# GLA's decayed keys and queries made in steps: from 4 tokens to 16, 64 and 128 by factors of a block

## The chip, the core and the metric

The program runs on one NeuronCore of a Trainium2 chip. Its engines are TensorE (PE; its weight loads are listed as PEld), VectorE (DVE), ScalarE (ACT), GpSimd (POOL) and SyncE (SP, which here only issues DMAs). Each engine works through its own list of instructions in order. The metric is the device time of one execution in microseconds (us); the kernel before takes 1629.36 us (median of 3 runs, 1627.66 to 1630.39).

## The reference

Two layers over 1024 tokens of width 1024: layer 0 mixes tokens by gated linear attention (GLA, 4 heads, key width 128, value width 512), layer 1 by a Mamba-2 mixer. Only GLA is touched. Within a chunk, with `b` the running sum of the log decays,

```python
    b = jnp.cumsum(ai, axis=-2)
    o_inter = jnp.einsum('bhcd,bhdv->bhcv', qi * jnp.exp(b), S)
    rel = jnp.where(causal, b[:, :, :, None, :] - b[:, :, None, :, :], -jnp.inf)
    attn = jnp.sum(qi[:, :, :, None, :] * ki[:, :, None, :, :] * jnp.exp(rel), axis=-1)
    o = o_inter + jnp.einsum('bhij,bhjv->bhiv', attn, vi)
    S = jnp.exp(b_last[:, :, 0, :, None]) * S + jnp.einsum(
        'bhjd,bhjv->bhdv', ki * jnp.exp(b_last - b), vi)
```

The sum over `d` has a decay that depends on both tokens and on `d`. It becomes a matmul only if the decay is split into a part for the key and a part for the query, each measured from a token between the two, so that neither exponential overflows.

## The kernel before

The 1024 tokens go in two halves of 512 (t = 0, 1); the first half meets each weight for the first time and splits it, the second loads the low part that the first has saved. GLA's work is the stage up to about 800 us of the span: four heads for t = 0, then four for t = 1. Every large product has three matmuls (high times high, low times high, high times low, lines 223 to 225 and 469 to 471). ACT makes a weight's high part `wh` (line 171), POOL its low part `wl` (line 176), or a DMA brings it. These matmul units of 12 run one behind the other, and a generator per head, `mixer(h)`, advances about one `yield` per unit beside them, so that its own small work falls between them. A scheduler that estimates times then fixes each engine's list; the kernel's `yield`s set the priorities.

A mixer projects the gate (z, line 540), makes `b` by four scans on DVE (line 551), and from `b`, the keys `k` and the queries `q` in a layout of 128 channels by 512 tokens: the keys decayed to the end of the chunk of 128 (`kd`, lines 558 to 560), the queries from its start (`qd`, 563 and 564), keys and queries about the chunk's middle (`d`, 569 to 573), keys to the end of each 16 and each 4 tokens (`keys`, 579 to 581), and queries against the end of each earlier 16, 4 or 1 tokens (`queries`, 597 to 601, with a copy on POOL for single tokens). Each takes a subtraction on DVE, an exponential on ACT and a multiplication on DVE; the tile names show up in the profile as `t`, `x`, `o` and `raw`, and `b` as `m`. PE then transposes `kd` (line 626), multiplies keys by queries (line 655), DVE places the results by masks (616, 620), and the attention and the state follow (705, 706, 712). At its end a mixer takes the norm over 512 values (line 293 on PE, 299 to 313 on DVE) and writes its output in four pieces `u` (line 738 on DVE), times the gate (739, POOL), rounded to `yh` and `yl` (743 on ACT, 744 on DVE), which the output projection reads. While one mixer ends, the next begins. DVE also carries values and gates out of PSUM (lines 480 and 419): a matmul that needs the bank waits for that.

## Time and profile before

| | us |
|---|---|
| median of the runs (lowest, highest) | 1629.36 (1627.66, 1630.39) |
| the profiled execution, whole time | 1634.13 |
| its span, first to last instruction | 1632.4 |
| PE busy | 1580.0 |
| DVE, ACT, POOL busy | 984.5, 947.2, 692.8 |

The profiled execution lies 4.8 us above the median of the runs. A matmul's busy time is modelled, and consecutive matmuls overlap. "Idle before" and a releaser name what ended an engine's wait. TensorE's granted clock is given as a share of 2.4 GHz.

### The profile page before, as it was taken

Reading aid. Unit: us, or ns where it says so; the run is one execution under the profiler, and the core shown is the slowest. Engines: PE = TensorE matmul, PEld = TensorE weight load, DVE = VectorE, ACT = ScalarE, POOL = GpSimd, SP = SyncE. Lnnn points to the kernel's source line nnn. Section 1 sums busy time; section 2 is a strip of 40 time slices with the busy share of each in tenths; the row PEclk is TensorE's granted clock in tenths of the full one; section 3 lists DMA queues with packets and bytes.
Section 4 is the critical chain, followed back from the end, with each engine's and each line's share of the span. In section 5 each row is a group of like instructions: output and inputs, shape, how many; then the busy total and the mean of one; then the engine's idle time right before and its main releaser. Section 6 shows DMA issues by size and latency. Waiting matters only on the chain.

```text
span 1632.4 us, 23995 instructions
## 1 busy us (share of the span) xinstructions
PE 1580.0 (97%) x8272; PEld 1308.2 (80%) x8272; DVE 984.5 (60%) x1579; ACT 947.2 (58%) x1788; POOL 692.8 (42%) x542
## 2 busy tenths in 40 slices
PE   7998999999999999999999999999999999999996
PEld 5777887877887888878888888887878888888886
DVE  6457567495736436295855534467885973355657
ACT  4435364543726355464874766665757777667843
POOL 6457566563412121126545655665523232222322
PEclk9999999999999999999999999999999999999999
DMA  7634556364585556463587555566666776656762
GB/s 232 185 123 131 176 174 201 123 201 146 191 269 193 162 166 217 154 207 120 176 262 228 175 188 173 173 209 216 208 193 186 257 235 221 204 177 189 260 197 84
DMA packets 172746, 309.30 MB, mean 189 GB/s; under 512 B 19088, under 2 KB 25104, under 8 KB 172624
## 3 DMA queue, kind: packets, MB, share of 16 engines
q1 hardware_dynamic: 172624, 307.77, 59.2%
q8 instruction: 65, 1.06, 0.3%
q14 instruction: 57, 0.47, 0.1%
HBM read 232.06 MB, written 75.63 MB: 188 GB/s over the span
## 4 chain that ended last, share of the span: by engine, by line
PE 78%; DVE 11%; ACT 4%; DMA 3%; issue 2%; POOL 2%; SPq 0%; DVEq 0%; ACTq 0%; POOLq 0%
PE pp L223 19%; PE pp L225 19%; PE pp L224 19%; PE pp L469 3%; PE pp L470 3%; PE pp L471 3%; PE mb L953 2%; PE mb L706 2%; DMA wraw<-w_in 2%; PE mb L705 2%; PE mb L946 1%; PE mb L655 1%; POOL wl L176 1%; PE mb L224 1%; PE mb L223 1%
## 5 line engine op out<-in xcount | busy, mean ns | idle before, releaser
L171 ACT CAST wh<-wraw 128x512 fp32r<-128x512 f32 x472 | 289.3, 618 | 379.3 <-PE pp L224 154.2
L223 PE MATMUL pp<-hh,wh 128*128 128x512 f32 x1184 | 468.3, 396 | 13.2 <-ACT wh L171 7.5
L176 POOL TENSOR_TENSOR wl<-wraw,wh 128x512 fp32r<-128x512 f32 x240 | 352.6, 1478 | 268.6 <-ACT wh L171 233.7
L224 PE MATMUL pp<-hl,wh 128*128 128x512 f32 x1184 | 464.1, 392 | 1.6 <-DVE hl L371 1.3
L225 PE MATMUL pp<-hh,wl 128*128 128x512 f32 x1184 | 463.2, 392 | 0.0
L223 PEld LDWEIGHTS pp<-hh,wh 128*128 128x128 f32 x1184 | 222.8, 188 | 65.3 <-ACT wh L171 9.0
L224 PEld LDWEIGHTS pp<-hl,wh 128*128 128x128 f32 x1184 | 222.9, 188 | 49.2 <-DVE hl L371 3.2
L225 PEld LDWEIGHTS pp<-hh,wl 128*128 128x128 f32 x1184 | 222.8, 188 | 46.5 <-issue 0.3
L223 PE MATMUL pp<-yh,wh 128*128 128x512 f32 x448 | 180.5, 403 | 5.2 <-DVE sg L419 2.4
L225 PE MATMUL pp<-yh,wl 128*128 128x512 f32 x448 | 178.5, 399 | 4.6 <-POOL wl L176 4.6
L224 PE MATMUL pp<-yl,wh 128*128 128x512 f32 x448 | 177.3, 396 | 0.0
L321 POOL TENSOR_TENSOR ss<-ss,t 128x512 f32<-128x512 f32 x53 | 74.4, 1403 | 81.7 <-ACT t L320 70.4
L223 PEld LDWEIGHTS pp<-yh,wh 128*128 128x128 f32 x448 | 85.6, 191 | 26.2 <-issue 4.5
L225 PEld LDWEIGHTS pp<-yh,wl 128*128 128x128 f32 x448 | 85.6, 191 | 24.4 <-POOL wl L176 5.1
L469 PE MATMUL pp<-wh,hh 128*128 128x512 f32 x256 | 100.8, 395 | 2.7 <-DVE m L444 2.7
L470 PE MATMUL pp<-wl,hh 128*128 128x512 f32 x256 | 101.0, 394 | 0.0
L471 PE MATMUL pp<-wh,hl 128*128 128x512 f32 x256 | 100.3, 394 | 0.0
L224 PEld LDWEIGHTS pp<-yl,wh 128*128 128x128 f32 x448 | 85.4, 191 | 18.2
L824 DVE SCALAR_TENSOR_TENSOR m<-pp,pr,m 128x509 f32<-128x509 f32 (+2 forms) x96 | 70.3, 742 | 40.0 <-ACT m L821 38.9
L824 DVE SCALAR_TENSOR_TENSOR x<-pp,pr,x 128x509 f32<-128x509 f32 (+2 forms) x96 | 71.2, 743 | 33.3 <-ACT x L821 32.2
L645 POOL TENSOR_TENSOR t<-v,t 128x512 fp32r<-128x512 f32 x28 | 40.6, 1460 | 101.5 <-ACT t L644 65.7
L739 POOL TENSOR_TENSOR t<-t,sg 128x512 f32<-128x512 f32 x32 | 50.9, 1621 | 75.3 <-ACT sg L98 68.3
(284 smaller groups left out, 2654.0 us busy)
## 6 DMA issues: line engine op xcount, KB each, us to landing
wraw<-w_in SPq DMA_DIRECT2D x352, 256.0 KB, 3.5
low_in<-wl SPq DMA_DIRECT2D x176, 256.0 KB, 3.8
wl<-low_in SPq DMA_DIRECT2D x176, 256.0 KB, 3.4
wraw<-w_out SPq DMA_DIRECT2D x128, 256.0 KB, 3.6
low_out<-wl SPq DMA_DIRECT2D x64, 256.0 KB, 4.3
v<-a_cum SPq DMA_DIRECT2D x64, 256.0 KB, 3.8
wl<-low_out SPq DMA_DIRECT2D x56, 256.0 KB, 3.4
xn<-x SPq DMA_DIRECT2D x43, 256.0 KB, 3.8
```

The lines of the kernel that those rows point to most:

```text
L171: A.copy(hi[:, 0:w], raws[n][:, 0:w])
L176: G.tensor_tensor(lo[:, 0:w], raws[n][:, 0:w], hi[:, 0:w].bitcast(F32), op=ALU.subtract)
L223: PE.matmul(o, lh, rh, start=first, stop=False)
L224: PE.matmul(o, lh, rl, start=False, stop=False)
L225: PE.matmul(o, ll, rh, start=False, stop=last)
L321: eng.tensor_tensor(ss, ss, sq, op=ALU.add)
L469: PE.matmul(o, rh[kb][:, cs], wh[:], start=(kb == 0), stop=False)
L470: PE.matmul(o, rh[kb][:, cs], wl[:], start=False, stop=False)
L471: PE.matmul(o, rl[kb][:, cs], wh[:], start=False, stop=(kb == KB - 1))
L645: G.tensor_tensor(vl, v[c], vh.bitcast(F32), op=ALU.subtract)
L739: G.tensor_tensor(u, u, self.g[h][vb], op=ALU.mult)
L824: V.scalar_tensor_tensor(dst[:, s:], o[:, 0:T - s], col(C_CW + j * 32 + si), dst[:, s:], op0=ALU.mult, op1=ALU.add)
```

## The change

`b` is turned into decays only over 4 tokens (and single tokens, as before). The keys to the end of 4 tokens, `k4`, are multiplied by a factor for each 4 tokens to give those to the end of 16, `k16`, and these by a factor for each 16 to give `kd` and the key half of `d`. The queries go the same way, in the tiles `t4` and `t16` (names `o1` and `o0`): queries from the last 4-token end, copies of them further back (`later`), then 16, then `qd` and the query half of `d`. The factors, 472 values per channel, are differences of `b` at block ends. POOL makes them: a copy of the ends (`ends`) and twelve small subtractions and copies per head; one exponential on ACT turns all of them into factors (`f`). The masks' placing keeps its instructions.

```diff
+            G.tensor_copy(ends[:, :, 1:9], b16[:, :, :, 15])
+            start, end = ends[:, :, 0:8], ends[:, :, 1:9]
...
+            fk = less(factors(NC, 8, 4), end.unsqueeze(3).to_broadcast([P, NC, 8, 4]), b4)
+            fq = factors(NC, 8, 4)
+            less(fq[:, :, :, 0], start, start)
+            less(fq[:, :, :, 1:4], b4[:, :, :, 0:3], start.unsqueeze(3).to_broadcast([P, NC, 8, 3]))
+            fkd = less(factors(NC, 8), ends[:, :, 8:9].to_broadcast([P, NC, 8]), end)
...
+            fqd = factors(NC, 8)
+            G.tensor_copy(fqd, start)
+            act(f[:, 0:at0[0]], f[:, 0:at0[0]], AF.Exp, scale=1.0 / 16)
...
+            k4 = tmp()
+            V.tensor_tensor(four(k4), bv[:, :, 3:4].to_broadcast([P, P, 4]), bv, op=ALU.subtract)
+            act(k4, k4, AF.Exp, scale=1.0 / 16)
+            yield
...
+            V.tensor_tensor(t4[:, :, 1:4, :], b5[:, :, 1:4, :], b5[:, :, 0:3, 3:4].to_broadcast([P, 32, 3, 4]),
+                            op=ALU.subtract)
+            V.tensor_tensor(t4[:, :, 0, :].rearrange("p (c j) l -> p c j l", c=NC), b16[:, :, :, 0:4],
+                            start.unsqueeze(3).to_broadcast([P, NC, 8, 4]), op=ALU.subtract)
+            act(t4[:, :, 0:4, :], t4[:, :, 0:4, :], AF.Exp, scale=1.0 / 16)
+            times(k4, k, k4)
+            k16 = tmp()
+            times(four(k16), four(k4), fk.rearrange("p c j m -> p (c j m)").unsqueeze(2).to_broadcast([P, P, 4]))
+            yield
             kd = tmp()
-            V.tensor_tensor(c3(kd), bc[:, :, P - 1:P].to_broadcast([P, NC, P]), bc, op=ALU.subtract)
-            act(kd, kd, AF.Exp, scale=1.0 / 16)
-            V.tensor_tensor(kd, k, kd, op=ALU.mult)
-            yield
-            qd = tl("x", 4)[:]
-            act(qd, b, AF.Exp, scale=1.0 / 16)
-            V.tensor_tensor(qd, q, qd, op=ALU.mult)
...
+            times(kd.rearrange("p (c j l) -> p c j l", c=NC, j=8), k16.rearrange("p (c j l) -> p c j l", c=NC, j=8),
+                  fkd.unsqueeze(3).to_broadcast([P, NC, 8, 16]))
+            times(t4[:, :, 0:4, :], q.rearrange("p (n m l) -> p n m l", m=4, l=4), t4[:, :, 0:4, :])
+            yield
...
+            times(t16[:, :, 0:4, :].rearrange("p n m (i l) -> p n m i l", l=4),
...
+            later(t4, f4, 4)
+            yield
...
-            k16, q16 = keys(16), queries(16, flat[0])
+            q1 = [singles(tl("raw", 2, (P, N_RAW))[:], 0, 2)]
             yield
...
-            k4, q4 = keys(4), queries(4, flat[1])
...
-            q1 = [queries(1, tl("raw", 2, (P, N_RAW))[:], 2 * i, 2 * i + 2) for i in range(2)]
+            q1.append(singles(tl("raw", 2, (P, N_RAW))[:], 2, NC))
```

A mixer has three `yield`s more between the scans and the products of keys and queries, so its later parts, and the end of a mixer against the beginning of the next, stand elsewhere in the lists. In the list after, line 535 is 532 before, 543 is 540, 554 is 551, 296 is 293, 700 is 626 and 724 is 655; `times` is line 599 and `less` line 577. The lists of the Mamba stage are the same.

First place: DVE's list, t = 1, the end of the third head's mixer (names `o_1268`, `o_1269` before) beside the copies of the fourth head's values `v` out of PSUM. Before:

```order
L313 SCALAR_TENSOR_TENSOR rstd_6519<-t_6523,t_6520 128x512
L738 SCALAR_TENSOR_TENSOR t_6550<-o_1268_5921,pr,rstd_6519 128x512
L738 SCALAR_TENSOR_TENSOR t_6575<-o_1268_5921,pr,rstd_6519 128x512
L738 SCALAR_TENSOR_TENSOR t_6609<-o_1269_5922,pr,rstd_6519 128x512
L738 SCALAR_TENSOR_TENSOR t_6634<-o_1269_5922,pr,rstd_6519 128x512
L480 COPY v_6599<-pp_6390 128x512
L480 COPY v_6603<-pp_6392 128x512
```

And now:

```order
L483 COPY v_6583<-pp_6358 128x512
L483 COPY v_6587<-pp_6360 128x512
L302 TENSOR_SCALAR t_6589<-mb_6559 128x512
L314 TENSOR_TENSOR t_6595<-t_6589,t_6592 128x512
L315 SCALAR_TENSOR_TENSOR t_6595<-t_6595,t_6592 128x512
L316 SCALAR_TENSOR_TENSOR rstd_6591<-t_6595,t_6592 128x512
L807 SCALAR_TENSOR_TENSOR t_6622<-o_1265_5902,pr,rstd_6591 128x512
```

The two copies stood behind the four `u`; now they stand ahead of the norm and of all four. Between the first and second and the second and third head of t = 1 they have moved in the same way.

Second place: DVE's list, t = 0, third head, up to the last instruction of `kd`, which is `t_2284` before and `t_2361` after. Before (the subtraction of `t_2284` is the fourth instruction behind the scans):

```order
L564 TENSOR_TENSOR x_2308<-m_376_1870,x_2308 128x512
L321 TENSOR_TENSOR ss_2191<-ss_2191,t_2319 128x512
L601 TENSOR_TENSOR raw_2448<-m_376_1870,raw_2448 128x64x3
L601 TENSOR_TENSOR raw_2448<-m_376_1870,raw_2448 128x64x2
L419 TENSOR_TENSOR sg_2280<-pp_2201,rstd_261 128x512
L560 TENSOR_TENSOR t_2284<-m_389_1930,t_2284 128x512
```

And now (`t_2285` is `f`, `t_2331` is `k16`, `o_478` is `t16`, `o_479` is `t4`):

```order
L617 TENSOR_TENSOR o_479_2326<-m_459_2242,ends 128x32x4
L599 TENSOR_TENSOR raw_2538<-m_365_1821,raw_2538 128x64
L599 TENSOR_TENSOR t_2298<-m_381_1882,t_2298 128x512
L599 TENSOR_TENSOR o_479_2326<-m_365_1821,o_479_2326 128x32x16
L599 TENSOR_TENSOR t_2331<-t_2298,t_2285 128x512
L599 TENSOR_TENSOR o_478_2325<-o_479_2326,t_2285 128x8x64
L599 TENSOR_TENSOR o_479_2326<-o_479_2326,t_2285 128x32x8
L599 TENSOR_TENSOR o_479_2326<-o_479_2326,t_2285 128x32x4
L422 TENSOR_TENSOR sg_2413<-pp_2346,rstd_263 128x512
L599 TENSOR_TENSOR t_2361<-t_2331,t_2285 128x512
```

`kd` now stands behind the single tokens' queries, `k4`, `t4`, `k16` and `t16`, and from `t_2331` on every instruction needs POOL's factors.

Third place: POOL's list, t = 0, second head. Before, low parts of weights follow one another; only the copy for single tokens stands between:

```order
L176 TENSOR_TENSOR wl_1364<-wraw_1283,wh_1363 128x512
L176 TENSOR_TENSOR wl_1393<-wraw_1312,wh_1392 128x512
L176 TENSOR_TENSOR wl_1422<-wraw_1337,wh_1421 128x512
L603 COPY raw_1551<-m_180_917 128x64x4
L176 TENSOR_TENSOR wl_1463<-wraw_1369,wh_1462 128x512
```

And now:

```order
L563 COPY ends<-m_281_1361 128x4x8
L577 TENSOR_TENSOR t_1392<-m_281_1361 128x64
L577 TENSOR_TENSOR t_1392<-m_281_1361 128x32
L179 TENSOR_TENSOR wl_1409<-wraw_1304,wh_1408 128x512
L577 TENSOR_TENSOR t_1392<-ends,m_281_1361 128x128
L577 TENSOR_TENSOR t_1392<-ends 128x32
L577 TENSOR_TENSOR t_1392<-m_281_1361,ends 128x32x3
L577 TENSOR_TENSOR t_1392<-ends 128x32
L577 TENSOR_TENSOR t_1392<-ends 128x16 x3
L577 TENSOR_TENSOR t_1392<-ends 128x8
L594 COPY t_1392<-ends 128x32
L179 TENSOR_TENSOR wl_1437<-wraw_1336,wh_1436 128x512
```

The copy of `ends` needs the scans on DVE, and every `wl` behind it now stands behind that. PE first needs `wl_1409` 99 matmuls of 512 columns behind the norm's matmul of the first head's mixer.

On PE, in matmuls of 512 columns, the lists have these distances to the transposes of `kd` and to the products of keys and queries, counted from the gate's projection z in the first head of t = 0 and from the norm's matmul of the mixer that ends in the other heads:

| head | transposes, products before | now |
|---|---|---|
| t = 0, first | 68, 88 | 79, 80 |
| t = 0, second | 112, 137 | 133, 170 |
| t = 0, third | 130, 171 | 134, 171 |
| t = 0, fourth | 122, 171 | 134, 171 |
| t = 1, second to fourth | 122 or 123, 171 | 134, 171 |

The output projection first reads `yh` 135 matmuls behind the norm's matmul before and 98 behind it now, for the first three heads of t = 1.

## Rows read from the trace of the kernel before

**Rows 1.** The page: busy time, share of the span and instructions of each engine; and the chain that ended last, its shares by engine.

```profile
PE 1580.0 (97%) x8272; PEld 1308.2 (80%) x8272; DVE 984.5 (60%) x1579; ACT 947.2 (58%) x1788; POOL 692.8 (42%) x542
...
PE 78%; DVE 11%; ACT 4%; DMA 3%; issue 2%; POOL 2%; SPq 0%; DVEq 0%; ACTq 0%; POOLq 0%
```

**Rows 2.** A stretch of 50 us that holds PE's longest wait in GLA's stage: its length, then PE busy (instructions), PEld, DVE, ACT, POOL, the granted clock, the DMA share and GB/s.

```profile
150.00:200.00 50.00, 45.34 (x256) 37.36 (x255) 35.09 (x70) 18.65 (x37) 30.64 (x20) 0.93 0.51 163
```

**Rows 3.** Who PE waited for in the whole run: us in total, times, longest us.

```profile
PE pp L225 <- POOL wl L176: 4.6, 1, 4.6
PE pp L223 <- DVE v L480: 4.2, 3, 1.4
PE mb L655 <- DVE raw L601: 3.4, 1, 3.4
...
PE mb L626 <- DVE t L560: 2.4, 2, 1.4
PE pp L223 <- DVE sg L419: 2.4, 2, 2.0
PE pp L223 <- DVE acc L515: 1.7, 2, 1.3
...
PE mb L655 <- DVE t L581: 0.5, 1, 0.5
...
PE mb L223 <- DVE a L620: 0.5, 1, 0.5
```

**Rows 4.** PE in order of time, start and us: the first head's z and the norms of the first three heads (t = 0); then, for t = 1, the third head's norm, the fourth's z, 37 matmuls behind it, and the matmul after that.

```profile
69.30 0.39 PE L540 MATMUL mb<-stp,wup 128*128 128x512 f32 x1
...
132.16 0.39 PE L293 MATMUL mb<-t,onr 128*128 128x512 f32 x1
...
217.01 0.39 PE L293 MATMUL mb<-t,onr 128*128 128x512 f32 x1
...
313.46 0.39 PE L293 MATMUL mb<-t,onr 128*128 128x512 f32 x1
...
688.74 0.39 PE L293 MATMUL mb<-t,onr 128*128 128x512 f32 x1
...
697.17 0.39 PE L540 MATMUL mb<-stp,wup 128*128 128x512 f32 x1
698.96 0.47 PE L223 MATMUL pp<-hh,wh 128*128 128x512 f32 x1 [1.41 <-DVE v L480]
```

**Rows 5.** DVE in order of time, fourth head of t = 1, where POOL has nothing to do: start and us of a group.

```profile
705.03 0.73 DVE L597 TENSOR_TENSOR raw<-m 128x192 f32<-128x192 f32 x3
705.67 0.68 DVE L558 TENSOR_TENSOR t<-m 128x512 f32<-128x512 f32 x1
706.28 0.68 DVE L569 TENSOR_TENSOR t<-m 128x512 f32<-128x512 f32 x1
...
707.48 2.09 DVE L597 TENSOR_TENSOR o<-m 128x384 f32<-128x384 f32 x6
...
715.38 0.85 DVE L601 TENSOR_TENSOR raw<-m,raw 128x192 f32<-128x192 f32 x3
```

**Rows 6.** DVE in order of time, t = 0: the first head from behind the scans to its last queries, and the scans of the second, third and fourth head.

```profile
74.26 1.78 DVE L597 TENSOR_TENSOR raw<-m 128x192 f32<-128x192 f32 x3
...
88.96 4.02 DVE L601 TENSOR_TENSOR raw<-m,raw 128x192 f32<-128x192 f32 x3
...
148.92 2.02 DVE L551 TENSOR_TENSOR_SCAN m<-t,t 128x128 f32<-128x128 f32 x4
...
236.36 2.58 DVE L551 TENSOR_TENSOR_SCAN m<-t,t 128x128 f32<-128x128 f32 x4
...
331.73 1.86 DVE L551 TENSOR_TENSOR_SCAN m<-t,t 128x128 f32<-128x128 f32 x4
```

**Rows 7.** POOL in order of time: the first head of t = 0 behind the scans, then the second; last, the one instruction of DVE in that second stretch that reads PSUM.

```profile
74.09 1.33 POOL L176 TENSOR_TENSOR wl<-wraw,wh 128x512 fp32r<-128x512 f32 x1 [0.63 <-ACT wh L171]
79.11 8.78 POOL L176 TENSOR_TENSOR wl<-wraw,wh 128x512 fp32r<-128x512 f32 x3 [3.68 <-ACT wh L171]
88.84 1.34 POOL L176 TENSOR_TENSOR wl<-wraw,wh 128x512 fp32r<-128x512 f32 x1 [0.96 <-DVE o L601]
90.14 2.71 POOL L645 TENSOR_TENSOR t<-v,t 128x512 fp32r<-128x512 f32 x2
...
152.35 10.78 POOL L176 TENSOR_TENSOR wl<-wraw,wh 128x512 fp32r<-128x512 f32 x3 [2.29 <-PE pp L225]
...
158.96 0.68 DVE L419 TENSOR_TENSOR sg<-pp,rstd 128x512 f32<-128x512 f32 x1
```

**Rows 8.** POOL's groups by line and shape, whole run: us busy, mean ns of one, idle before.

```profile
L176 POOL TENSOR_TENSOR wl<-wraw,wh 128x512 fp32r<-128x512 f32 x240 | 352.6, 1478 | 268.6 <-ACT wh L171 233.7 <-PE pp L225 9.2 <-DMA wraw<-w_in 7.0
...
L838 POOL TENSOR_TENSOR m<-m,heads 128x3 f32<-128x3 f32 x16 | 3.6, 227 | 51.5 <-DVE m L824 51.5
...
L834 POOL TENSOR_TENSOR heads<-halo,pr 128x96 f32<-128x96 f32 x1 | 0.4, 361 | 3.8 <-ACT halo L827 3.8
```

**Rows 9.** DVE in order of time, t = 1, the four `u` of the third head and the two copies behind them.

```profile
693.40 4.81 DVE L738 SCALAR_TENSOR_TENSOR t<-o,pr,rstd 128x512 f32<-128x512 f32 x4
698.14 1.28 DVE L480 COPY v<-pp 128x512 f32<-128x512 f32 x2
```

More of the change, by code (lines that the diff above doesn't have):

```diff
@@ L584, in queries, with later @@
-            def queries(s, e, c0=0, c1=NC):
-                w, n = 4 * s, (c1 - c0) * P // (4 * s)
-                own = 4 if s == 1 else 0
-                e = e[:, 0:n * (6 * s + own)].rearrange("p (n w) -> p n w", n=n)
-                cs = slice(c0 * P, c1 * P)
-                bv, qv = c3(b[:, cs], w), c3(q[:, cs], w)
+            def later(t, f, s):
+                w = t.shape[1]
+                for o, n, g in ((4, 2, f[0]), (6, 1, f[1])):
+                    g = g.rearrange("p c j m -> p (c j) m").unsqueeze(3).to_broadcast([P, w, n, s])
+                    times(t[:, :, o:o + n, :], t[:, :, 4 - n:4, :], g)
@@ L592, in queries @@
                 after = []
                 for i in range(3):
-                    f, l = (i + 1) * s, 4 * s
-                    o = sum(4 * s - (m + 1) * s for m in range(i))
-                    after.append((e[:, :, o:o + l - f], f))
-                    V.tensor_tensor(after[-1][0], bv[:, :, f:l], bv[:, :, f - 1:f].to_broadcast([P, n, l - f]),
+                    o = (0, 3, 5)[i]
+                    after.append(e[:, :, o:o + 3 - i])
+                    V.tensor_tensor(after[i], bv[:, :, i + 1:4], bv[:, :, i:i + 1].to_broadcast([P, n, 3 - i]),
@@ L618, in place, with put @@
-                if s == 1:
-                    m = msk[:, m0 + 3 * nm:m0 + 3 * nm + 4 * nm].rearrange("p (n w) -> p n w", n=n)
-                    V.copy_predicated(dst, m, src[:, :, o:o + 4])
+                m0, n = QUARTERS[s]
+                dst = a64[:, c0:c1, :].rearrange("p c w -> p (c w)").rearrange("p (n m l) -> p n m l", n=n, l=s)
+                msks = [msk[:, m0 + i * n:m0 + (i + 1) * n].unsqueeze(2) for i in range(4 if s > 1 else 7)]
+                def put(m, mask, src):
+                    V.copy_predicated(dst[:, :, m:4, :], mask.unsqueeze(3).to_broadcast([P, n, 4 - m, s]), src)
```

102 lines of the change are left out of this document (66 added, 36 removed).

## The prediction

> **What bounds the kernel now.** I read the page first: PE is busy for 97% of the span and the chain that ended last runs over PE for 78% and over DVE for 11% [rows 1]. So work taken from DVE, ACT or POOL is worth nothing by itself; it counts where PE waits. The list of PE's waits gives those places [rows 3]. For GLA's heads of t = 0 they are 3.4 us for the last single-token queries (`raw`, first head), 4.6 for one weight's low part from POOL (second head), and in the third and fourth head 2.4 for `kd`, 2.4 for a gate in PSUM, 1.7, 0.5 and 0.5 for other late instructions of DVE: 15.5 us. For t = 1 they are three waits of 1.4 us, 4.2 in all, for the copies of `v`. Then I read DVE and POOL in order of time around them. In the fourth head of t = 1, where POOL is idle, DVE's work from behind the scans to the last `raw` goes from 705.03 to 716.23, 11.2 us without a gap [rows 5]. The same list in the first head of t = 0 goes from 74.26 to 92.98, 18.7 us [rows 6]; one extra gate evacuation explains 0.6 of the 7.5 us between them. In these 18.7 us POOL runs seven products [rows 7], some 1.33 us each when free, 9.3 us: 6.9 of them came out of DVE's time, three quarters. So in t = 0 DVE and POOL get in each other's way, and PE waits for what comes last.
>
> **The waits for `v`, t = 1.** The copies stood behind four `u` that take 4.81 us [rows 9]; PE's next matmul came 1.41 us late for it [rows 4]. In the list after they stand ahead of the norm, and nothing is queued ahead of them but work that is done earlier. The `u` move behind the copies by 1.2 us; the output projection first needs their results 98 matmuls of 0.228 us, 22.3 us, after the norm, and before, all of it and the next scans were done 16.3 us after it (688.74 to 705.03 [rows 4, 5]). I take all of 4.2 us as gained; the bounds are 4.2 and nothing, should another late instruction of DVE take over the bank's release.
>
> **DVE's work per head.** Per head, the list before has 22 instructions between scans and products that the change touches, the list after 15; ACT's eight exponentials of 256 to 768 columns become three. ACT's part I cost at nothing: ACT is busy 58% of the span and PE waits for DVE, not for it [rows 1, 3]. What matters is when `kd` is ready for the transposes, now that `kd` comes late. From the pitches of rows 5 (three single-token subtractions 0.64 us, a product of 512 columns 0.60, subtractions of 384, 256 and 128 columns about 0.47, 0.33 and 0.20, three single-token products 0.85) the list after, up to `kd`, is 0.64 + 0.47 + 0.64 + 0.20 + 0.60 + 0.85 + 0.85 for the differences and the single tokens, 4 x 0.60 for `k4`, `t4`, `k16`, `t16`, 0.53 for the copies further back and 0.60 for `kd`: 7.8 us. With what else stands between (one gate 0.60 in the second head; a `yl` and two gates 1.8 in the third and fourth; gate, `qd` and 0.53 in the first) it is 9.5, 8.4, 9.6 and 9.6 us in the four heads of t = 0.
>
> **POOL's work.** The trace has no factor instruction. The nearest rows are POOL's products of 3 and of 96 columns, 0.227 and 0.361 us [rows 8]. Thirteen of them cost 3.0 to 4.7 us; most are of 32 columns or fewer, so I take 0.27 each, 3.5 us. One or two `wl` stand among or right behind them, 2.8 us at the mean of free and disturbed ones, 6.3 us together. Between none and all of it lands on DVE; at the three quarters of the first head, 4.7 us. The exponential of the factors I cost at nothing, since DVE has the products of `k4` and `t4` to do meanwhile; without that cover it is one exponential more, about a product's 0.6 us.
>
> The State Buffer page of the Trainium skill ("SBUF — State Buffer", Who interferes with whom) says that a DVE instruction with two SBUF inputs and a GpSimd instruction that reads SBUF exclude each other, and the second fully blocks until the first finishes. Here the `wl` at 152.35 [rows 7] waited for more than one: its group took 10.78 us where three free ones take 4.0, and it was DVE's evacuation of PSUM at 158.96 that let it in, behind a row of DVE products that issued back to back. By the page's rule each factor instruction would wait for one DVE product at most; what that gives is a rival below.
>
> **`kd` against the transposes, t = 0.** A matmul's pitch is 0.228 us (688.74 to 697.17 for 37 [rows 4]). First head: z at 69.30, transposes now 79 matmuls later, 87.3; DVE is behind the scans at 74.26, which leaves 13.0 us, against 9.5 + 4.7 = 14.2: PE waits 1.2. Second: from the norm at 132.16 to the end of the scans at 150.94 are 18.8 us [rows 4, 6]; 133 matmuls are 30.3, which leaves 11.5 against 13.1: 1.6. Third: 217.01 to 238.94 are 21.9, less 0.6 as one `yl` has moved behind the scans; 134 matmuls are 30.6, which leaves 9.3 against 14.3: 5.0. Fourth: 313.46 to 333.59, 20.1 less 0.6, which leaves 11.1 against 14.3: 3.2. Together 11.0, where the waits were 15.5: 4.5 gained. The products follow 37 matmuls (8.4 us) behind the transposes, one in the first head, where only 0.3 to 0.7 us of `d` is left then; they add nothing. The other waits of rows 3 in the third and fourth head (gates, `acc`) come from the same late DVE, and I let the wait at the transposes stand for them.
>
> **The same for t = 1.** 688.74 to 705.03 are 16.3 us; 134 matmuls leave 14.3, and `kd` needs 7.8 plus three quarters of 3.5, 10.4. No wait, with 3.9 us to spare; I allow 1 us for all four heads.
>
> **The low parts behind POOL's factors.** POOL now waits for the scans before it makes further `wl`. In the second head the first matmul that needs the `wl` between the factors stands 99 matmuls behind the norm, 22.6 us, 3.8 us after the scans; three factor instructions and a product are 2.1. That is bare, and I cost it at nothing because the same lateness of DVE is already counted at the transposes.
>
> **The clock.** After the 4.6 us wait the granted clock fell: its mean is 0.93 in that stretch [rows 2], that is 14% of it at 1.2 GHz instead of 2.4, a loss of 3.5 us. I take nothing for it, since waits of like length remain; 3.5 us is the bound to either side.
>
> The sum: 4.2 + 4.5 - 1.0 = 7.7 us. The profiled execution would come to 1634.1 - 7.7 = 1626.4; it lies 4.8 us above the median of the runs, and so the median would be 1621.7 us.
>
> **Rivals.** (a) Slower: POOL's factors starve. If DVE's products run back to back as they did beside the `wl` at 152.35, POOL gets in only when DVE itself stops for the factors, some 5 to 7 us behind the scans; then come 3.5 + 2.8 us of POOL, the exponential, and 2.3 to 2.9 us up to `kd`, some 16 us instead of 14.3, and the `wl` behind them come some 7 us late in the second head as the one at 152.35 did. With 3, 7, 6.5 and 5 us at PE in the four heads, 21.5, plus 3.5 at the lower clock, less 15.5 and the 4.2 of `v`, it is 5.3 us slower: 1634.7. It decides where `kd` needs over 16 us on the mean of four heads. For it speaks row 152.35, against it that most new products wait for an earlier one of DVE or ACT, which leaves POOL an opening. (b) The t = 0 waits nearly vanish: if each factor instruction waits for at most one product, the factors are there before DVE asks, POOL costs it less than the difference of 18.7 and 11.2, and 15.5 + 4.2 + 3.5 less some 3 gives 1609. The page's rule above would have it so. Against it: the third head has only 9.3 us for 9.6 us of DVE work. (c) Nothing is gained on balance: the waits at the transposes replace those of t = 0 at the same size plus a few at t = 1, and the saved work of DVE and ACT was hidden anyway: 1628.
>
> **How the numbers follow.** The forecast has 0.46, (a) 0.20, (b) 0.13, (c) 0.21. By itself the forecast reaches from 1616 to 1626, by the bounds of POOL's share (none to all of 6.3 us in four heads, of which PE sees a part). What a measurement of this kernel can tell from no change is about 0.2%, 3.3 us. Faster: nearly all of the forecast, (b) and a little of (c), 0.57; the same: the rest of these two and a little of (a), 0.23; slower: 0.20. The range from 1611 to 1636 leaves out the tail of (b) and the far side of (a).
>
> **What would show it.** PE's list of waits has no wait for `v` in t = 1; the largest waits of t = 0 are at the transposes, for `kd`, longest in the third head; DVE is busy some 22 us less (8 heads, 11.2 and 1.2 for the old `k4` before, 7.8, 0.6 for `qd`, 0.53 and about 0.67 for `d` now) and ACT less too, with PE's busy time as before; POOL's thirteen instructions per head last some 0.27 us each where DVE is quiet and longer beside its products. It is wrong if the transposes never wait (b), if PE waits for `wl` in the second to fourth head (a), or if `v` still holds PE up.

## The result and the profile after

The changed kernel takes 1634.57 us (median of 9 runs, 1631.49 to 1637.92), the kernel before 1629.72 us on the same chip (9 runs, 1627.66 to 1631.25). The ratio is 1.0029 with a 95% interval from 1.0017 to 1.0040: some 5 us slower, where the prediction was 8 us faster. One execution of 5602.42 us, of the version with `kd` direct below, is a slow one and left out of its median and ratio.

The page of the changed kernel, busy time of the engines and the chain that ended last, answers to [rows 1]:

```profile
PE 1583.6 (97%) x8272; PEld 1312.5 (80%) x8272; DVE 978.8 (60%) x1523; ACT 922.8 (57%) x1746; POOL 714.0 (44%) x639
...
PE 70%; DVE 15%; DMA 6%; ACT 4%; issue 3%; POOL 1%; SPq 1%; DVEq 0%; ACTq 0%; POOLq 0%
```

ACT has 24 us less to do, POOL 21 more, and DVE, which lost 56 instructions, only 5.7 less. DVE's share of the chain has risen. Whom PE waited for (us in total, times, longest us) answers to [rows 3]:

```profile
PE mb L700 <- DVE t L599: 16.9, 4, 6.0
...
PE mb L296 <- DVE t L293: 1.1, 1, 1.1
...
PE mb L876 <- DVE t L864: 0.5, 1, 0.5
```

The three waits for `v` are gone. All but 1.5 us of what the heads of t = 0 wait for now stands at the transposes, for `kd`. Two small waits are new, L876 and L296: the first transposes of the stage that follows, and the last head's norm. Over all of GLA's stage, from 60 to 840 us, PE's waits add up to 20.8 us before and 20.7 after: what went at some places came at others. PE in order of time shows the places; the number in brackets is the wait:

```profile
90.44 1.11 PE L700 MATMUL mb<-ident,t 128*128 128x128 f32 x4 [3.46 <-DVE t L599]
...
163.32 0.66 PE L700 MATMUL mb<-ident,t 128*128 128x128 f32 x4 [3.37 <-DVE t L599]
...
262.11 1.11 PE L700 MATMUL mb<-ident,t 128*128 128x128 f32 x4 [5.95 <-DVE t L599]
...
360.02 1.11 PE L700 MATMUL mb<-ident,t 128*128 128x128 f32 x4 [4.13 <-DVE t L599]
...
789.77 0.80 PE L876 MATMUL mb<-ident,t 32*128 32x32 f32 x10 [0.52 <-DVE t L864]
...
792.39 0.50 PE L296 MATMUL mb<-t,onr 128*128 128x512 f32 x1 [1.13 <-DVE t L293]
```

Stretches of 50 us of the changed kernel (columns as in [rows 2], the granted clock third from the right):

```profile
50.00:100.00 50.00, 46.54 (x243) 36.62 (x241) 30.84 (x56) 19.40 (x33) 28.22 (x32) 0.93 0.52 165
150.00:200.00 50.00, 45.62 (x244) 36.68 (x243) 31.00 (x53) 15.65 (x29) 31.64 (x31) 0.97 0.53 170
250.00:300.00 50.00, 44.05 (x238) 36.48 (x237) 36.31 (x61) 20.42 (x38) 29.68 (x28) 0.93 0.60 195
350.00:400.00 50.00, 45.40 (x254) 35.25 (x253) 39.08 (x66) 20.47 (x40) 21.27 (x17) 0.97 0.58 193
750.00:800.00 50.00, 48.34 (x244) 37.73 (x243) 35.61 (x47) 25.28 (x53) 29.13 (x20) 0.97 0.48 154
```

The clock fell after each of the four waits, and once more at the handover to the next stage. In the kernel before, the stretches beside that of [rows 2] (0.93) are these:

```profile
50.00:100.00 50.00, 46.63 (x249) 36.43 (x248) 34.67 (x65) 22.49 (x40) 29.39 (x21) 0.97 0.54 167
250.00:300.00 50.00, 48.04 (x273) 40.24 (x273) 33.76 (x59) 20.73 (x40) 26.35 (x20) 0.97 0.63 194
350.00:400.00 50.00, 46.87 (x271) 36.88 (x270) 35.07 (x60) 20.76 (x41) 20.24 (x15) 0.97 0.59 198
750.00:800.00 50.00, 50.00 (x257) 40.06 (x256) 35.56 (x50) 28.53 (x51) 28.24 (x21) 1.00 0.46 144
```

A mean of 0.93 in 50 us is 3.5 us lost, 0.97 is 1.5, so before lost 8.0 us over the five stretches and the changed kernel 11.5.

Where `kd` comes late is read from DVE and POOL in the third head of t = 0, from the end of the scans at 245.77 on. DVE:

```profile
243.15 2.62 DVE L554 TENSOR_TENSOR_SCAN m<-t,t 128x128 f32<-128x128 f32 x4
...
252.07 1.80 DVE L606 TENSOR_TENSOR t<-m 128x512 f32<-128x512 f32 x1
...
256.89 1.76 DVE L599 TENSOR_TENSOR t<-t,t 128x512 f32<-128x512 f32 x1
258.57 2.28 DVE L599 TENSOR_TENSOR o<-o,t 128x512 f32<-128x512 f32 x3
260.77 0.68 DVE L422 TENSOR_TENSOR sg<-pp,rstd 128x512 f32<-128x512 f32 x1
261.38 2.08 DVE L599 TENSOR_TENSOR t<-t,t 128x512 f32<-128x512 f32 x2
```

and POOL beside it:

```profile
245.83 0.28 POOL L563 COPY ends<-m 128x32 f32<-128x32 f32 x1 [0.96 <-DVE m L554]
246.08 0.74 POOL L577 TENSOR_TENSOR t<-m 128x64 f32<-128x64 f32 x2
247.88 1.40 POOL L179 TENSOR_TENSOR wl<-wraw,wh 128x512 fp32r<-128x512 f32 x1 [1.05 <-issue]
...
250.49 1.10 POOL L577 TENSOR_TENSOR t<-ends 128x32 f32<-128x32 f32 x5
251.54 0.41 POOL L594 COPY t<-ends 128x32 f32<-128x32 f32 x1
251.91 1.41 POOL L179 TENSOR_TENSOR wl<-wraw,wh 128x512 fp32r<-128x512 f32 x1
255.13 1.29 POOL L179 TENSOR_TENSOR wl<-wraw,wh 128x512 fp32r<-128x512 f32 x1 [1.81 <-ACT wh L174]
256.65 1.44 POOL L179 TENSOR_TENSOR wl<-wraw,wh 128x512 fp32r<-128x512 f32 x1 [0.24 <-ACT wh L174]
258.73 1.64 POOL L179 TENSOR_TENSOR wl<-wraw,wh 128x512 fp32r<-128x512 f32 x1 [0.64 <-ACT wh L174]
261.79 1.39 POOL L179 TENSOR_TENSOR wl<-wraw,wh 128x512 fp32r<-128x512 f32 x1 [1.42 <-ACT wh L174]
```

POOL's small instructions (twelve: ten subtractions and two copies, where the change's text and the prediction speak of thirteen) are over 6.2 us behind the scans. Then the low parts go on, and a DVE instruction beside one takes up to 1.1 us longer: 1.80 at 252.07, 1.76 at 256.89. The same list in the fourth head of t = 1, where POOL makes no low parts, has no such row, and its `kd` is the first of the two at 721.89, some 9.8 us behind the scans (end 712.72) and not 16.3 (the first of the two at 261.38):

```profile
711.36 1.36 DVE L554 TENSOR_TENSOR_SCAN m<-t,t 128x128 f32<-128x128 f32 x4
...
715.60 0.70 DVE L606 TENSOR_TENSOR t<-m 128x512 f32<-128x512 f32 x1
...
721.89 1.02 DVE L599 TENSOR_TENSOR t<-t,t 128x512 f32<-128x512 f32 x2
```

### The profile page after: what moved, and what is told of

It reads as the page before. It is cut to its first block, busy times and chain, and to the rows that moved or that the text cites. A ratio compares the mean times of both kernels' runs of the same rounds, so it can differ in the third digit from the quotient of the medians.

```text
span 1633.0 us, 24046 instructions
## 1 busy us (share of the span) xinstructions
PE 1583.6 (97%) x8272; PEld 1312.5 (80%) x8272; DVE 978.8 (60%) x1523; ACT 922.8 (57%) x1746; POOL 714.0 (44%) x639
## 4 chain that ended last, share of the span: by engine, by line
PE 70%; DVE 15%; DMA 6%; ACT 4%; issue 3%; POOL 1%; SPq 1%; DVEq 0%; ACTq 0%; POOLq 0%
PE pp L226 16%; PE pp L227 16%; PE pp L228 16%; PE pp L472 4%; PE pp L473 4%; PE pp L474 4%; DMA v<-a_cum 2%; PE mb L775 2%; PE mb L724 1%; PE mb L774 1%; PE mb L1022 1%; DMA x<-acc 1%; DMA wraw<-w_in 1%; DVE x L893 1%; PE mb L1015 1%
## 5 line engine op out<-in xcount | busy, mean ns | idle before, releaser
L179 POOL TENSOR_TENSOR wl<-wraw,wh 128x512 fp32r<-128x512 f32 x240 | 336.1, 1409 | 261.6 <-ACT wh L174 227.2
L227 PEld LDWEIGHTS pp<-hl,wh 128*128 128x128 f32 x1184 | 223.6, 189 | 48.3 <-DVE hl L374 1.6
L1104 POOL TENSOR_TENSOR t<-t,o 128x512 fp32r<-128x512 f32 x32 | 42.5, 1329 | 93.8 <-ACT o L1102 91.8
```

The source lines that it names most:

```text
L179: G.tensor_tensor(lo[:, 0:w], raws[n][:, 0:w], hi[:, 0:w].bitcast(F32), op=ALU.subtract)
L227: PE.matmul(o, lh, rl, start=False, stop=False)
L1104: G.tensor_tensor(xel[-1], xe, hi.bitcast(F32), op=ALU.subtract)
```

## The experiments

After the result there were three candidates for the loss: POOL's work beside DVE (its factors, or its low parts), `kd`'s place at the end of the chain, and the order, because a head has three steps (`yield`) more. Times are medians, ratios are to the kernel before on the same chip; "waits" are PE's from 60 to 425 us, where the heads of t = 0 lie, summed over the list of waits.

| run | us | ratio, 95% interval | waits, t = 0 |
|---|---|---|---|
| before | 1629.7 | | 16.6 |
| changed | 1634.6 | 1.0029 (1.0017 to 1.0040) | 18.4 |
| factors on DVE | 1633.5 | 1.0022 (1.0011 to 1.0034) | 18.1 |
| kd direct | 1631.1 | 1.0010 (0.9994 to 1.0026) | 19.2 |
| transposes later | 1636.5 | 1.0047 (1.0030 to 1.0063) | 18.6 |
| before, three more steps | 1642.6 | 1.0079 (1.0054 to 1.0104) | 24.3 |
| three steps out behind the products | 1633.5 | 1.0028 (1.0017 to 1.0039) | 20.0 |
| three steps out ahead of them, transposes later | 1630.2 | 1.0001 (0.9992 to 1.0010) | 17.4 |
| kd direct, three steps out | 1626.7 | 0.9977 (0.9966 to 0.9988) | 15.1 |
| steps at rate 1.05 | 1633.2 | 1.0020 (1.0010 to 1.0030) | 18.7 |
| changed, low parts left out | 1613.0 | 0.9881 (0.9864 to 0.9897) | 10.0 |
| before, low parts left out | 1606.1 | 0.9841 (0.9823 to 0.9859) | 7.9 |
| changed, kd ahead of single tokens | 1632.5 | 1.0011 (0.9999 to 1.0023) | 18.0 |
| kd direct, three steps out, kd first | 1626.4 | 0.9966 (0.9950 to 0.9981) | 15.4 |
| changed, last head at rate 1.05 | 1631.4 | 1.0001 (0.9989 to 1.0013) | 19.0 |
| kd direct, three steps out, v on ACT | 1622.4 | 0.9952 (0.9938 to 0.9966) | 15.3 |
| kd direct, three steps out, half low parts on DVE | 1614.5 | 0.9901 (0.9885 to 0.9917) | 6.7 |
| before, half low parts on DVE | 1615.1 | 0.9906 (0.9890 to 0.9922) | 7.4 |
| changed, half low parts on DVE | 1617.0 | 0.9910 (0.9893 to 0.9926) | 8.1 |
| kd direct, three steps out, both edits | 1609.5 | 0.9871 (0.9855 to 0.9887) | 7.3 |

**Factors on DVE.**

```diff
-                G.tensor_tensor(o, x, y, op=ALU.subtract)
+                V.tensor_tensor(o, x, y, op=ALU.subtract)
```

(and the copies of `ends` and `fqd`; all twelve small instructions of a head).

> The thirteen factor instructions and two small copies per head run on DVE, behind the scans, and POOL keeps only its weights' low parts and products; PE's order is that of the changed kernel. Theory W (kd is late in t = 0 because of POOL's low parts of weights beside DVE's new chain, of which the prediction counted too few; the factors themselves cost about what was said): DVE takes some 13 x 0.2 to 0.25 = 3 us more per head and is freed of the 3 us of factors on POOL, so kd comes within 1 us of where it came, the waits at the transposes add up to 14 to 20 us again (16.9 in the changed kernel) and the time is 1632 to 1638 us. Rival F (the factors starve on POOL and hold the chain up): kd comes 2 to 3 us sooner, the four waits shrink to 6 to 10 us, 1624 to 1628 us.

1633.5 us; the waits at the transposes are 12.6 us, a little under the 14 to 20 named, and other late instructions took up the rest, 18.1 in all. `kd` came 0.9 us sooner on the mean of the four heads of t = 0 (15.4 us from the end of the scans to the transposes, 16.4 in the changed kernel). So it is not the place of the factors, POOL instead of DVE, that made the kernel slower; what they cost at either place this run doesn't show.

**kd made directly, and the transposes later.** The first takes `kd` out of the chain, the second moves the transposes two steps on, behind the last `singles`:

```diff
+            kd = tmp()
+            V.tensor_tensor(c3(kd), bc[:, :, P - 1:P].to_broadcast([P, NC, P]), bc, op=ALU.subtract)
+            act(kd, kd, AF.Exp, scale=1.0 / 16)
+            times(kd, k, kd)
             k4 = tmp()
...
-            times(kd.rearrange("p (c j l) -> p c j l", c=NC, j=8), k16.rearrange("p (c j l) -> p c j l", c=NC, j=8),
-                  fkd.unsqueeze(3).to_broadcast([P, NC, 8, 16]))
```

> One part undone: kd is again made by its own subtraction, exponential and product right behind the scans, all the rest stays as changed; PE's order is that of the changed kernel but for the first head. Theory K (the whole loss sits in kd's place at the end of the chain of k4, k16, kd): the waits at the transposes of t = 0 go (16.9 us) and with them the stretches of low clock behind them; 0.6 to 1.2 us more DVE work per head may leave 0 to 2 us at the products in the third and fourth head; 1612 to 1620 us. Rival N (DVE is late as a whole in t = 0 and something else takes the wait's place at the products): the waits add up to 10 us or more again, now at the products, and the time is 1626 to 1634 us.

> Order alone: the same instructions as in the changed kernel, but the transposes of kd stand two steps of the generator later, some 24 matmuls or 5.5 us later in PE's list (in the first head they stay where they were, one matmul ahead of the products). Theory K: the waits of 3.4, 6.0 and 4.1 us in heads 2 to 4 fall to 0, 0.5 and 0 us and that of the first head stays at 3.5; 12 us and some 3 to 5 us of low clock less: 1617 to 1623 us. Rival N (as above): DVE is late for the products too, 3 us or more per head wait there; 1626 to 1634 us.

1631.1 and 1636.5 us: theory K fell. N had the first time right (the second is above its range) and the place wrong, since it is not the products that mostly wait but the matmuls that need a bank back. PE's waits from 60 to 840 us with `kd` made directly:

```profile
PE pp L226 <- DVE sg L422: 14.5, 5, 4.0
...
PE mb L700 <- DVE t L598: 0.7, 1, 0.7
```

The 16.9 us at the transposes are 0.7, and 14.5 us for `sg`, the gate's evacuation from PSUM, have come in their place (14.7 us with the transposes later). DVE's list is late as a whole; PE meets it at one instruction or at the next. Keeping the twelve single-token instructions behind `kd` on DVE is one dependency more:

```diff
+                    tc.add_manual_dep(m.ins, made.ins.name, ORDER, reason="singles")
```

(`m` is a single-token subtraction, `made` the product that makes `kd`.)

> The changed kernel with one edge of order more: the single-token differences (twelve DVE instructions with their products, some 4 us) may not be put ahead of kd on DVE. PE's order as in the changed kernel but for the first head (transposes 65, products 87 matmuls behind z). If kd's place at the end of DVE's list is all that counts (theory K): the waits at the transposes fall from 16.9 to under 4 us, 1617 to 1623 us. If DVE is late as a whole in t = 0 (theory N, by the earlier run with kd made directly): gates and products wait for 12 us or more in its stead, 1629 to 1635 us.

1632.5 us, with `sg` for 3.2 and 4.3 us in the second and fourth head and 3.6 at the third's transposes: theory N by the time and by the 18.0 us of waits that stay, though the transposes' part fell from 16.9 to 5.4.

**The order alone.** The kernel before, its own computation, with three more `yield` between the parts:

```diff
             V.tensor_tensor(kd, k, kd, op=ALU.mult)
             yield
+            yield
             qd = tl("x", 4)[:]
...
             V.tensor_tensor(qd, q, qd, op=ALU.mult)
+            yield
...
             V.tensor_tensor(dv[:, :, 64:P], c3(q)[:, :, 64:P], dv[:, :, 64:P], op=ALU.mult)
+            yield
```

> The kernel before with its own computation of keys and queries, and only the three more steps of the generator that the changed kernel has, so that the transposes stand 121 and the products 170 matmuls behind z instead of 85 and 134. Theory O (the order is worth more than the saved work): kd is early and 36 more matmuls, 8.2 us, lie ahead of the products; the three waits of 1.4 us for v go, and of the 15.5 us of t = 0 the 3.4 us of the first head stay, the rest goes mostly: 1614 to 1622 us. Rival H (the new order itself costs what was lost, at the handover to the next stage and by work that it moves together): 1628 to 1636 us.

1642.6 us, 12.2 us slower than the kernel before: three empty steps cost more than the whole change does, and more than either theory allowed. PE's waits from 60 to 840 us:

```profile
PE pp L225 <- POOL wl L176: 13.3, 3, 6.9
PE pp L223 <- DVE sg L419: 7.1, 3, 3.5
PE mb L657 <- DVE raw L603: 4.4, 1, 4.4
PE pp L224 <- DVE yl L746: 2.9, 1, 2.9
PE mb L293 <- DVE t L290: 1.1, 1, 1.1
PE mb L809 <- DVE t L797: 0.5, 1, 0.5
```

One step is worth about one unit of 12 matmuls, so three put a head's norm, `u` and `yl` 36 matmuls later, while the projections stay where they are: from the norm to the output projection that reads `yl` there are 98 matmuls instead of 135, as in the changed kernel (now PE waits 2.9 us for `yl`), and `u`, `yl`, the next scans and the gates crowd on DVE. The waits rose by 8.5 us (29.3 for 20.8), those for POOL's low parts the most (13.3 for 4.6), and the granted clock is 0.93 in each of the four stretches from 50 to 100, 150 to 200, 250 to 300 and 350 to 400 us: 14.0 us lost, for 8.0 before. The new computation stands that order (with its transposes 12 matmuls further on) 8 us better than the old one (1634.6).

**The old number of steps with the new computation.** In the first run three `yield` were taken out behind the products:

```diff
             place(1, p1[1], 0, 2)
-            yield
             place(4, p4)
...
-            yield
             place(16, p16)
...
-            yield
             box = []
```

In the next two they were taken out ahead of the transposes, and the second also has the transposes later, the third `kd` direct:

```diff
             act(k4, k4, AF.Exp, scale=1.0 / 16)
-            yield
...
             times(four(k16), four(k4), fk.rearrange("p c j m -> p (c j m)").unsqueeze(2).to_broadcast([P, P, 4]))
-            yield
...
             later(t4, f4, 4)
-            yield
```

The fourth keeps the steps and raises the mixer's rate:

```diff
-            mix = mixq(g, h, 1.5 if h == p == 0 else 0.95)
+            mix = mixq(g, h, 1.5 if h == p == 0 else 1.05)
```

> The changed kernel with three steps of its generator taken out behind the products (two between the placings and one ahead of the head's norm), so that a head has as many steps as before: z, transposes and products stand where the changed kernel has them (133 and 170 matmuls behind z), but the norm stands 135 matmuls ahead of the output projection, as before, and no longer 99. Theory O (the three steps push each head's norm, its u and yl 36 matmuls closer to the output projection and into the next head's start, and that costs what the kernel before lost with three more steps, some 12 us, while the new computation by itself gains some 8): DVE has 8 us more for u, yl and the scans, so the waits at the transposes fall from 16.9 to under 6 us and the wait at the handover to the next stage goes; 1618 to 1625 us. Rival C (the new computation is worth nothing by itself, kd comes too late at any place of the norm): waits of 12 us or more, 1629 to 1636 us.

> The changed kernel with the three steps taken out ahead of the transposes, and these moved to 13 matmuls ahead of the products (121 behind z, products 134 behind z, norm 135 ahead of the output projection, as in the kernel before). Theory O: the order is that of before but for the transposes; kd is there some 14 to 16 us behind the scans, 0 to 2 us late per head of t = 0; 1620 to 1628 us. Rival C: 1629 to 1636 us, with waits at the transposes or for gates of 15 us or more.

> As the last, but kd is made directly behind the scans and the transposes stand 97 matmuls behind z: the closest to the kernel before's order with the new computation of everything else. Theory O: the 8 us between the kernel before with three more steps (1642.6) and the changed kernel (1634.6) come off the kernel before: 1618 to 1626 us. Rival C: 1629 to 1636 us.

> The changed kernel with all its steps, but the generator of a head is stepped 1.05 times per unit of projection work instead of 0.95, so that 28 steps take as many units as 25 did: norm 135 matmuls ahead of the output projection, transposes 121 and products 158 behind z (in one head of t = 1 z itself comes 37 matmuls sooner). Theory O: 1618 to 1627 us, without the wait at the handover. Rival C: 1629 to 1636 us.

1633.5, 1630.2, 1626.7 and 1633.2 us. The first, second and fourth lie in the range of rival C, the third between the two ranges. Theory O is right in direction where transposes and products return to their places too (`kd` direct is faster with the old number of steps than with the new one, by 4.4 us in the medians and 5.4 in the ratios), and too high in size; moving the norm back alone gives nothing: the waits for `v` come back with it (6.8 us for DVE's and 4.5 for ACT's copies in the first run) and 7.4 us for `sg` remain (from 60 to 840 us). `kd` made directly with the old number of steps beats both kernels, the one before by 0.2%. With the dependency on `kd`'s product added:

> The fastest version so far (kd made directly, as many steps as before, 1626.7 us, with waits at the transposes of 1.5, 5.1, 3.8 and 0.5 us) with the same edge of order: kd ahead of the single tokens on DVE. Theory K: these 11 us go, 1612 to 1619 us. Theory N: other late work of DVE takes their place, 1623 to 1629 us.

1626.4 us: its waits at the transposes fell from 11.0 to 1.4 us and instead came 7.0 us at the products (`raw`) and 3.2 for `sg` (1.6 without the dependency). Theory N again.

**POOL's low parts left out.** In t = 0 they are loaded from the low part of an earlier weight; so part of the computation is left out:

```diff
+                if lows and key[0] in ("in0", "out0"):
+                    dma(lo[:, 0:w].bitcast(F32), next(iter(lows.values()))[:])
+                else:
-                G.tensor_tensor(lo[:, 0:w], raws[n][:, 0:w], hi[:, 0:w].bitcast(F32), op=ALU.subtract)
+                    G.tensor_tensor(lo[:, 0:w], raws[n][:, 0:w], hi[:, 0:w].bitcast(F32), op=ALU.subtract)
```

> Leaves work out: in the changed kernel the low parts of GLA's weights in t = 0 are not made on POOL (but for the first few); each is loaded instead, from the low part of one earlier weight, so that PE and DVE do the same work and DMA moves some 120 pieces of 256 KB more. Theory P (in t = 0 kd is late because POOL's products stretch DVE's chain: 14.1 to 17 us from the scans to kd, against 9.8 in t = 1, where low parts are loaded anyway): the 16.9 us at the transposes fall below 2 us and nothing of size takes their place; with less time at the low clock 1610 to 1618 us. Rival D (DVE's own list is too long for the place that it has, with or without POOL): 8 us or more of waits stay in t = 0; 1622 to 1630 us.

> The same left out of the kernel before. Theory P: its 15.5 us of waits in t = 0 go as well, the three waits for v of 1.4 us stay, the norm stands as before: 1611 to 1618 us, within 3 us of the changed kernel without low parts, so that the change is worth little where POOL is quiet. Rival D: 1620 us or more, and the changed kernel without low parts is faster by 4 us or more since its lists on DVE are shorter.

1613.0 and 1606.1 us: theory P by the times, some 22 and 25 us. Not all of this lies in the heads: the first head's z starts at 62.84 and 63.03 us, 6 us sooner than with the low parts (68.91 and 69.30), and from there to the last head's z 15.2 and 14.4 us are gained. Of the 16.9 us at the transposes 1.7 are left, and 4.4 of the 10.0 us that PE still waits in t = 0 (rival D named 8 or more) are for the added loads. The kernel before came out 5 us under the time expected: with POOL's low parts gone the change costs 6.9 us, not under 3; that this is the order's price, with little to set against it, is not shown. `kd` in the changed kernel without low parts is ready 10.4, 11.0, 12.2 and 11.1 us behind the scans, for 16.5, 15.7, 16.3 and 16.9 with them, so the low parts cost the chain 5.2 us per head on the mean. In the fourth head (the scans end at 323.66, and the transposes start as soon as `kd` is there):

```profile
322.29 1.37 DVE L557 TENSOR_TENSOR_SCAN m<-t,t 128x128 f32<-128x128 f32 x4 [5.57 <-ACT t L98]
...
334.75 0.66 PE L703 MATMUL mb<-ident,t 128*128 128x128 f32 x4 [0.96 <-DVE t L602]
```

The pages, first the changed kernel without low parts:

```profile
PE 1575.1 (98%) x8272; PEld 1305.9 (81%) x8272; DVE 918.8 (57%) x1523; ACT 922.6 (57%) x1746; POOL 556.0 (35%) x530
```

and the kernel before without them:

```profile
PE 1571.0 (98%) x8272; PEld 1304.7 (81%) x8272; DVE 936.2 (58%) x1579; ACT 946.8 (59%) x1788; POOL 520.7 (32%) x433
```

DVE issues the same 1523 instructions and is busy 60.0 us less, for 109 low parts: 0.55 us each. In the kernel before it is 48.3 us, 0.44 each.

**The handover.** Only the last head of t = 1 at rate 1.05:

```diff
-            mix = mixq(g, h, 1.5 if h == p == 0 else 0.95)
+            mix = mixq(g, h, 1.5 if h == p == 0 else 1.05 if h == GH - 1 and p else 0.95)
```

> The changed kernel, but the last head of t = 1 alone is stepped 1.05 times per unit instead of 0.95, which brings its norm back to 42 matmuls sooner (2866 matmuls from the start instead of 2908). Theory H (the three more steps push the last head's norm into the start of the next stage, where the norm, transposes and the clock behind them cost 3 us): the waits of 1.1 and 0.5 us at the handover go, and the time falls from 1634.6 to 1630.5 to 1632.5 us. Rival: nothing at the handover counts to the end, since the next stage waits there for something else: 1633.5 to 1636 us.

1631.4 us, 3.2 less (4.6 by the ratios); the waits at L876 and L296 are gone. Theory H.

**v on ACT, and half of the low parts on DVE.** Both on the version with `kd` direct and the old number of steps:

```diff
-                                elif c % 2:
-                                    V.tensor_copy(vt, banks[c][:])
...
-                G.tensor_tensor(lo[:, 0:w], raws[n][:, 0:w], ...
+                (V if n % 2 and key[0] in ("in0", "out0") else G).tensor_tensor(lo[:, 0:w], raws[n][:, 0:w], ...
```

> The version with kd made directly and as many steps as before (1626.7 us), with all copies of v in t = 1 on ACT instead of every second one on DVE. Its waits for v (1.0 and three of 1.4 us) stand behind DVE's u. If they count in full: 1621.5 to 1623.5 us. Rival: ACT, which has the exponential and logarithm of the norm and the gates there, makes v as late as DVE did: 1625 to 1628 us.

> The same version, with every second low part of GLA's weights in t = 0 made on DVE (0.6 us each when undisturbed) instead of POOL (1.3 us, and up to 1.1 us that a DVE product beside it takes longer). Theory S (the price is the sharing: each low part on POOL costs DVE more than making it itself): t = 0's waits fall from some 13 us to 6 or less, 1616 to 1622 us. Rival T (it is the place in the queue: low parts on DVE stand behind or ahead of the chain, and PE waits for them or for the chain): 1627 to 1640 us, with waits for wl from DVE.

1622.4 us: 4.3 less, so the three waits of 1.4 us count about in full (the two intervals just touch). And 1614.5 us, 12.2 less (theory S, a little under its range). The pages of the version without and with half of the low parts on DVE:

```profile
PE 1571.9 (97%) x8272; PEld 1305.8 (81%) x8272; DVE 970.2 (60%) x1531; ACT 930.9 (57%) x1756; POOL 711.1 (44%) x631
```

```profile
PE 1574.1 (97%) x8272; PEld 1306.7 (81%) x8272; DVE 983.3 (61%) x1587; ACT 930.6 (58%) x1756; POOL 644.2 (40%) x575
```

56 products moved. At 0.60 us by DVE's pitch they are 34 us, in this run their rows add up to 46.9, and DVE is busy only 13.1 us more: 20 to 34 us came back from its other instructions. Then the same edit in both kernels, and both edits together:

> The kernel before with every second low part of GLA's weights in t = 0 made on DVE and nothing else changed. Theory S (sharing is the price, whatever computes keys and queries): most of the 15.5 us of t = 0 go, 1614 to 1622 us. Rival (the gain of the last version needs the shorter lists of the new computation, since DVE has no room for the low parts in the old one): 1625 to 1635 us.

> The changed kernel with every second low part on DVE. By theory S its waits at the transposes shrink to under 8 us, the handover stays, 1617 to 1625 us, that is 2 to 6 us behind the same edit of the kernel before by the handover and the norm's place. Rival (the new computation has more room on DVE): at or below the kernel before with the same edit.

> kd made directly, as many steps as before, v on ACT, half of the low parts on DVE: if the two edits are independent, 1614.5 less 4.2: 1609 to 1612 us. If what one gives back is waited for elsewhere: 1613 to 1616 us.

1615.1, 1617.0 and 1609.5 us: the kernel before, with this one edit, is 15 us faster. The changed kernel is 2.0 us behind it (the intervals overlap, so the sign of these 2 us is open). The two edits add up; the last version is 1.3% faster than the kernel before.

## Why the prediction was wrong

- **The waits for `v`: right.** They are gone, and they are worth about 4 us, as the run with `v` on ACT shows from the other side. What the prediction did not see is that the price is paid elsewhere by the same move: the copies came free because norm and `u` went 36 matmuls back.
- **`kd` against the transposes: the mechanism right, one term too small, and this is the step that failed.** Predicted 1.2, 1.6, 5.0, 3.2 us, measured 3.5, 3.4, 6.0, 4.1: every place, and the third head longest, but 16.9 us for 11.0. DVE's own work was put at 9.5, 8.4, 9.6 and 9.6 us and POOL's part at 4.7; from the end of the scans to the transposes' start it took 16.5, 15.7, 16.3 and 16.9, so POOL's part, as what is left over DVE's own, was 7.0, 7.3, 6.7 and 7.3. The term was "three quarters of 6.3 us", with one or two low parts among the factors; POOL's list in time shows six or seven starting before `kd` is done, and a later `kd` leaves the stretch open to more of them. The run without low parts tells the two apart: the low parts cost the chain 5.2 us per head, where three quarters of 2.8, 2.1 us, were put for them, and some 1.9 us are left for the factors, where three quarters of 3.5, 2.6 us, were put. (On POOL the twelve instructions take 3.9 to 4.9 us per head, and not 3.5.) So it is the number of low parts that was mis-sized.
- **The one wait standing for the others: right.** Runs with `kd` early or the transposes late put 14.5 and 14.7 us on `sg` instead.
- **The old waits of t = 0 were taken as replaced** by 11.0 us at the transposes. They had come from the low parts on POOL (the kernel before without them keeps 7.9 us of waits in t = 0, none for `raw`, `kd` or gates), which the change leaves as they are; t = 0 waits 18.4 us for 16.6.
- **t = 1: right.** 9.8 us to `kd` for 10.4, no wait.
- **The low parts behind the factors: right** at nothing; PE never waits for one in the heads.
- **The clock: taken at nothing, bound 3.5 us; it was 3.5:** 2.0 more in the first and in the third head and 1.5 at the handover, 2.0 less in the second.
- **The handover: missing in the sum.** It is worth 3.2 us. The prediction went through the heads' transposes, products and output projections, and not the last head's norm, which the same three steps push into the next stage.
- **DVE busy 22 us less: wrong,** 5.7. The instructions went: without low parts DVE is busy 17.4 us less than in the kernel before without them (918.8 and 936.2). But the low parts stretch the new products more than the old ones, by 60.0 us for 48.3.

So the forecast, 8.7 us for the heads and `v` without the allowance for t = 1, shrinks by 5.9 at the transposes, 2.2 in small waits, 3.5 at the clock and 1.6 at the handover's waits; 1.1 us of old waits for ACT's copies of `v`, which it left out, went. That is 3.4 us slower, where the medians say 4.9. The three terms that failed are POOL's low parts, the clock and the handover, the first of them the largest.

The two profiled executions lie only 1.1 us apart (1634.1 and 1635.2), and PE's order of time shows where. In the changed kernel the first head's z, the last head's and a norm of the next stage stand here:

```profile
68.91 0.39 PE L543 MATMUL mb<-stp,wup 128*128 128x512 f32 x1
...
697.11 0.40 PE L543 MATMUL mb<-stp,wup 128*128 128x512 f32 x1
...
1137.23 0.40 PE L295 MATMUL mb<-t,onr 128*128 128x512 f32 x1
```

The first two are those at 69.30 and 697.17 [rows 4]; the norm before is this:

```profile
1136.25 0.40 PE L292 MATMUL mb<-t,onr 128*128 128x512 f32 x1
```

From the first z to the last it is 627.9 us before and 628.2 after: in these two profiles the heads came out even, with two of the three waits for `v` in the stretch, where some 6 us were to be gained. From the last z to the norm it is 439.1 and 440.1. Eight profiles with the handover's waits took 436.1 to 440.1 us there, 438.5 on the mean, and eleven others without them 433.3 to 438.0, 435.3 on the mean: 3.2 us, as the run with the last head's rate says. The profile of the kernel before is the one long exception, without these waits, in a stretch where the change does nothing; why is not known.

Rival (a) had the time, 1634.7 us, and its condition was met: `kd` took 16.4 us on the mean. Its mechanism was not the one at work: POOL got in between DVE's products all the time, the factors were made within 6 to 8 us of the scans with low parts among them, and on DVE they left the time as it was. So that it met the time is luck. Rival (b) would need POOL's products to cost DVE less than the trace of before allowed. Here the Trainium skill ("SBUF — State Buffer", Who interferes with whom) and the rows agree on the size of one encounter: a DVE instruction with two SBUF inputs waits for one POOL instruction, 1.1 us more at 252.07 where a low part takes 1.3 to 1.4. The rule gives no count, and the count is what the sum missed.

What stays open: how the cost of three more steps splits between crowding before the output projection and the places of transposes and products. It is 12.2 us with the old computation and 4.4 to 5.4 with `kd` direct, of which the handover is 3.2; the two runs that moved only the norm back (1633.5, 1633.2) mix it with the returning waits for `v`.

## What to carry to other kernels

Count what the other engine really runs beside a chain over the whole time that the chain is open, not what stands next to it in the list; here the low parts were the price before and after, and moving half of them to the engine they disturbed won 15 us, which no change of the chain tried here did. A step added to a generator is a change of order everywhere: time the old computation with empty steps before crediting the new one. And when a wait goes, look who comes next in the same late queue: `kd`, `sg`, `raw` and `v` took each other's place in t = 0, 15 to 20 us in all, through nine more orders of the new computation.

## What the runs showed of the hardware

A POOL product of 512 columns with operands in SBUF lengthens DVE's own instructions by 0.44 to 0.55 us on the mean of 109 (the runs without low parts), and by 1.1 us where it meets one. Making it on DVE cost a net 13.1 us for 56, 0.23 us each in busy time: the engine that is "too busy" was cheaper than the idle one. It goes the other way too: in the kernel before, the first of the three low parts at 152.35 [rows 7] took 7.8 us, where a free one takes 1.3, beside DVE products that followed one another without a gap:

```profile
L176 POOL TENSOR_TENSOR wl<-wraw,wh x1: 7811/7811/7811, 152.3 to 152.3; 128x512 fp32r<-128x512 f32 x1
```

Stretches at the lower of the two clock levels (1.2 instead of 2.4 GHz) followed all four waits of 3.4 to 6.0 us in the changed kernel, but also two waits of 0.5 and 1.1 us close together at 790, with ten small transposes and two matmuls between them, each at 1.5 to 3.5 us by the granted clock of its stretch. After the three waits of 1.4 us for `v` in the kernel before, each by itself, the granted clock stayed at 1.00 (475 to 525, 575 to 625 and 675 to 725 us).
